# Second layer rebuilt: projections in seven-product pairs through DRAM, memory attention after them, one scan over 64 groups

## The chip, the cores and the metric

The kernel runs on one core of a Trainium2 chip. The metric is the device time of one execution in microseconds (us), lower is better. A core has five engines with instruction streams of their own: TensorE (PE, matmul), VectorE (DVE), ScalarE (ACT), GpSimd (POOL) and SyncE (SP), which here only issues DMAs. Each engine works through its instructions in order, and waits on semaphores for others.

## The reference

Two layers over 1024 tokens of 1024 features, all in fp32. Each layer normalizes, projects, runs a sequence mixer (layer 0 gated linear attention, layer 1 S5) and a four-head cross-attention into 256 memory tokens, gates both with silu(z) and adds the output product to the residual. What the change touches is layer 1:

```python
h = rms_norm(x, norm_w[1])
u, z, xq = split_cols(h @ w_in, [2048, 3072, 1024])
...
# S5: 128 groups of 16 inputs and 64 complex states
x_t = Ab * x_{t-1} + Bb @ u_t            # per group, complex
y_t = Re(C @ x_t)
...
y = gelu(y + d * u)
y = y * sigmoid(y @ w_glu + b_glu)
...
xa = memory_attention(xq, mem_n, w_kv)   # softmax(q k^T / 16) v
x = x + (concat(y, xa) * silu(z)) @ w_out
```

## The kernel before, in words

Activations lie as [feature, token]: a tile has 128 features on the partitions and a half of 512 tokens. A product in fp32 is made of three matmuls on parts of 12 bits, high x high, high x low and low x high (`mm3`). The parts come from `split`: a cast on ACT (L69), which gives the high part, and a subtraction on DVE (L70), which gives the low part. `unit()` loads a block of 128 output features of a weight (128x1024, 512 KB) and splits it; `gemm` then needs 24 matmuls for a half of the tokens.

All DMAs are issued from SP's queue, in one order. The order on each engine and queue comes from a planner: the framework simulates the program when it is built and fixes each engine's order by that; on the chip every engine and queue keeps to it. A tile comes from a pool of a few buffers by tag, and a new tile waits until the readers of the tile that it replaces are done. PSUM has three banks of tag `mm`, two of `a` and one each of `b`, `o` and `s`.

S5 is computed over chunks of eight tokens: 128 chunks. For a group there is an operator from a chunk's inputs to its state (`s5_input_operator`, to `rt_d`), one from inputs to outputs (`s5_operators`, to `tp_d`) and one from the chunk's first state to outputs (`s5_output_operator`, to `o_d`). All are made of POOL instructions mostly; each call covers eight groups. The state goes from chunk to chunk by a scan on DVE of 127 steps.

The stages of the profiled execution, in us from its start:

- 0 to 950: layer 0 up to its output product of the memory branch (`w_out_memory`).
- 950 to 1242: the other two thirds of that product (`w_out`). After each of its blocks `between()` builds one of 16 `s5_operators` and, for n < 8 (`EARLY`), an output operator. `done()` normalizes a half of the tokens for layer 1 and stores them in a permuted order ("p s c": token in the chunk, then chunk).
- 1242 to 1592: `mem_attention` of layer 1. For each head a: two units of queries, two of gates (z), then `each(a)`, which builds four input operators and the late output operators on POOL, and stores them from SP (L743, L763), then scores, softmax and values. The gated output (L321) is stored from SP as well.
- 1592 to 2019: `s5`, in two parts of 64 groups. For each part: inputs `w_su` (eight units, to `ud` in DRAM and back as `uu`), the states before the scan (L835), then the scan (L862 to L866) in two chains of 16 groups, so that one chain's operation lies between two of the other. While part 0 is scanned PE projects the inputs of part 1; while part 1 is scanned it makes the outputs of part 0 (L887, L888). Then outputs of part 1 and the gates `w_sz[0:16]`.
- 2019 to 2651: the GLU, which needs all of S5's outputs (tiles `x200h` and so on), the output product of layer 1, the last norm.

Of the kernel before, what the change touches and what calls it, by code (L numbers as in the profile page):

```python
# [16 lines left out]
P = 128  # L17
# [14 lines left out]
class Tags:  # L32
    """A tile pool for each tag, so that a tile waits for the tiles it replaces and no others."""
# [12 lines left out]
class Trunk:  # L46
# [8 lines left out]
    # ---------------------------------------------------------------- helpers  # L55
# [19 lines left out]
    def unit(self, src):  # L75
        """A block of 1024 weight columns per partition, split into its two 12-bit parts."""
# [7 lines left out]
    def mm3(self, out, ah, al, bh, bl, first, last):  # L84
        mm = self.nc.tensor.matmul
        mm(out, ah, bh, start=first, stop=False)  # L86
        mm(out, ah, bl, start=False, stop=False)  # L87
        mm(out, al, bh, start=False, stop=last)  # L88

    def gemm(self, out, u, xs, first=True, last=True):  # L90
        """out[f, tok] += sum over the eight k tiles of u[k, f] * xs[k][k, tok]."""
        h, l = u
        n = len(xs)
        for k in range(n):
            s = slice(k * P, (k + 1) * P)
            self.mm3(out, h[:, s], l[:, s], xs[k][0], xs[k][1], first and k == 0, last and k == n - 1)

# [15 lines left out]
    def stats(self, pool, xs, width):  # L113
        """1 / RMS over features of xs[k] = [feature, token]."""
# [16 lines left out]
    def rstd(self, pool, tot, width):  # L131
        """From sums of squares, 1 / RMS: by column of 128 tokens, and along tokens over all partitions."""
# [13 lines left out]
    def norm(self, pool, xs, wcol, width, emit):  # L146
        """RMS norm over features: xs[k] is [feature, token]; emit(k, tile) takes the result."""
# [7 lines left out]
    def norm_in_place(self, pool, xs, wcol, width, emit, last):  # L155
        """As norm(), in place, and away from the vector engine unless it's the last one."""
# [92 lines left out]
    def silu2(self, pool, out, ps, tag="zt", bufs=2):  # L249
        """out = 2 * silu(ps)"""  # L250
# [4 lines left out]
    def mem_attention(self, qp, late, pool, kv, wx, wz, xs, y_out, each=lambda a: None):  # L255
        nc = self.nc
        kt = vv = None
        for a in range(4):
            q, z = {}, {}

            def queries(us, hf):
                for f in range(2):
                    ps = self.ps()
                    self.gemm(ps, us[f], xs[hf])
                    q[f, hf] = [qp.tile([P, HALF], F32R, tag="xq" + i, name="xq" + i, bufs=4 if self.layer else 5) for i in "hl"]
# [12 lines left out]
            if a == 0 and self.layer == 1:  # L278
                uz = units(wz)
                gates(uz, 0)  # L280
                gates(uz, 1)
                queries(units(wx), 1)
            else:
                queries(us, 1)
                us = units(wz)
                gates(us, 0)
                gates(us, 1)
            if kt is None:
                kt, vv = kv()
            each(a)  # L290
# [846 lines left out]
```

## Time and profile before

| what | value |
|---|---|
| three runs | 2660.28, 2652.02, 2657.59 us; median 2657.59 |
| the profiled execution | span 2651.5 us, 32793 instructions |
| PE / weight loads | 2479.2 us (94%) / 2058.8 us (78%) |
| DVE / ACT / POOL | 1271.8 (48%) / 846.4 (32%) / 525.7 us (20%) |
| DMA moved | 376.5 MB, mean 142 GB/s |

The profile holds one execution of its own; its span runs from its first to its last instruction, and the median of the three timed runs is 6.1 us above it. The matmuls of PE are pipelined: a record of 0.39 us starts every 0.23 us, so their busy time is the union of the records. "Idle before" in a group is the time in which the engine stood still just before an instruction of the group, and the name behind the arrow is what ended it.

### The profile page before, as it was taken

What the parts mean: (1) busy time and instruction counts of PE and PEld (TensorE: products, weight loads), DVE (VectorE), ACT (ScalarE), POOL (GpSimd) and SP (SyncE); (2) the same over time, 40 slices, a digit from 0 to 9 for tenths busy, and PEclk for the clock granted to TensorE, in tenths of its full rate; (3) what the DMA queues carried; (4) which work ended last, traced back from release to release, by engine and by line L of the source; (5) the groups of instructions that cost most, each with busy time, mean ns of one, the idle gap of its engine ahead of it and who ended that gap; (6) DMA issues with size and microseconds to landing.
All of it is one profiled execution on the core that took longest, in us unless ns stands there. A gap on an engine that the chain in (4) does not pass through costs nothing.

```text
span 2651.5 us, 32793 instructions
## 1 busy us (share of the span) xinstructions
PE 2479.2 (94%) x12000; PEld 2058.8 (78%) x12000; DVE 1271.8 (48%) x3270; ACT 846.4 (32%) x1424; POOL 525.7 (20%) x557
## 2 busy tenths in 40 slices
PE   7999999999999986999997639999999999999998
PEld 6888878888888874777785438888888888888887
DVE  7554353636364533255642211899964222243455
ACT  5422242525253312255421103333234111121144
POOL 6200000000000055676675640000000000000015
PEclk9999999999999997899998779999999999999999
DMA  6612121221213365475453335557668333355434
GB/s 228 188 46 74 52 72 64 74 70 63 81 56 125 114 213 171 140 229 183 165 182 113 124 115 183 167 163 237 220 223 274 123 119 119 119 175 194 136 127 159
DMA packets 198914, 376.50 MB, mean 142 GB/s; under 512 B 17409, under 2 KB 82561, under 8 KB 198753
## 3 DMA queue, kind: packets, MB, share of 16 engines
q1 hardware_dynamic: 198752, 374.41, 43.4%
q8 instruction: 94, 1.54, 0.2%
q14 instruction: 68, 0.55, 0.1%
HBM read 275.12 MB, written 95.55 MB: 140 GB/s over the span
## 4 chain that ended last, share of the span: by engine, by line
PE 33%; DMA 12%; POOL 8%; DVE 6%; issue 3%; SPq 1%; ACT 1%; POOLq 0%; DVEq 0%; ACTq 0%
PE ps_mm L88 10%; PE ps_mm L86 10%; PE ps_mm L87 10%; DMA od<-op 5%; DMA ipw<-ip_d 2%; DVE pd L862 2%; DMA rt<-op 2%; PE ps_a L835 1%; DVE st L866 1%; POOL op L742 1%; DMA par<-in_s_par 1%; POOL op L759 1%; POOL opt L760 1%; DVE pd L864 1%; POOL op L740 1%
## 5 line engine op out<-in xcount | busy, mean ns | idle before, releaser
L86 PE MATMUL ps_mm<-X,wh 128*128 128x512 f32 (+1 forms) x2496 | 970.7, 389 | 32.1 <-ACT X L69 26.9
L88 PE MATMUL ps_mm<-X,wl 128*128 128x512 f32 (+1 forms) x2496 | 968.9, 389 | 5.1 <-DVE wl L70 5.0
L87 PE MATMUL ps_mm<-X,wh 128*128 128x512 f32 (+1 forms) x2496 | 968.7, 388 | 2.6 <-DVE X L70 1.5
L86 PEld LDWEIGHTS ps_mm<-X,wh 128*128 128x128 f32 x2496 | 473.7, 190 | 127.8 <-ACT X L69 28.5
L88 PEld LDWEIGHTS ps_mm<-X,wl 128*128 128x128 f32 x2496 | 473.6, 190 | 100.6 <-DVE wl L70 8.7
L87 PEld LDWEIGHTS ps_mm<-X,wh 128*128 128x128 f32 x2496 | 473.3, 190 | 98.3 <-DVE X L70 5.1
L70 DVE TENSOR_TENSOR wl<-wr,wh 128x1024 fp32r<-128x1024 f32 x258 | 333.6, 1294 | 438.9 <-ACT wh L69 378.9
L69 ACT CAST wh<-wr 128x1024 fp32r<-128x1024 f32 x258 | 271.2, 1051 | 667.9 <-PE ps_mm L87 545.1
L125 POOL TENSOR_TENSOR nacc<-nacc,nsq 128x512 f32<-128x512 f32 (+1 forms) x42 | 56.8, 1353 | 995.6 <-ACT nsq L123 994.8
L862 DVE TENSOR_TENSOR pd<-a,st 128x64 f32<-128x64 f32 x508 | 139.9, 276 | 3.5 <-ACT st L839 1.7
L490 POOL TENSOR_TENSOR rs<-ss,mhalf 128x1 f32<-128x1 f32 x32 | 20.3, 633 | 601.3 <-DVE ss L488 601.3
L252 ACT ACTIVATE zt<-ps_mm 128x512 f32<-128x512 f32 x96 | 57.0, 594 | 233.6 <-PE ps_mm L88 209.3
L253 DVE SCALAR_TENSOR_TENSOR zs<-zt,ps_mm 128x512 f32<-128x512 f32 x96 | 65.3, 681 | 100.1 <-ACT zt L252 98.2
L866 DVE TENSOR_TENSOR st<-st,pd 128x32 f32<-128x32 f32 x508 | 107.4, 212 | 2.0
L70 DVE TENSOR_TENSOR X<-yr,X 128x512 fp32r<-128x512 f32 x96 | 72.4, 780 | 74.9 <-ACT X L69 68.8
L864 DVE TENSOR_TENSOR pd<-pd 128x32 f32<-128x32 f32 x508 | 95.2, 188 | 1.9
L86 PE MATMUL ps_b<-pth,kvh 128*128 128x512 f32 x32 | 14.5, 454 | 86.5 <-DVE y L321 86.0
L321 DVE SCALAR_TENSOR_TENSOR y<-ps_b,zs 128x512 f32<-128x512 f32 x32 | 22.1, 690 | 138.5 <-DMA y<-y 116.4
L69 ACT CAST X<-yr 128x512 fp32r<-128x512 f32 x96 | 58.0, 620 | 92.1 <-DMA yr<-y 76.0
L936 DVE SCALAR_TENSOR_TENSOR sg<-sg,y 128x512 f32<-128x512 f32 x32 | 22.0, 688 | 127.1 <-ACT sg L933 127.1
L86 PEld LDWEIGHTS ps_b<-pth,kvh 128*128 128x128 f32 x32 | 6.7, 211 | 89.3 <-DVE y L321 87.3
L87 PE MATMUL ps_mm<-wl,X 128*128 128x512 f32 x192 | 75.0, 391 | 0.0
(413 smaller groups left out, 3566.6 us busy)
## 6 DMA issues: line engine op xcount, KB each, us to landing
wr<-in_w_out SPq DMA_DIRECT2D x72, 512.0 KB
yr<-y SPq DMA_DIRECT2D x96, 256.0 KB
wr<-in_w_gv SPq DMA_DIRECT2D x32, 512.0 KB
wr<-in_w_glu SPq DMA_DIRECT2D x32, 512.0 KB
wr<-in_w_gz SPq DMA_DIRECT2D x24, 512.0 KB
wr<-in_w_sz SPq DMA_DIRECT2D x24, 512.0 KB
wr<-in_w_k SPq DMA_DIRECT2D x16, 512.0 KB
wr<-in_w_v SPq DMA_DIRECT2D x16, 512.0 KB
```

The lines of the kernel that those rows point to most:

```text
L69: nc.scalar.copy(h, src)
L70: (eng or nc.vector).tensor_tensor(l, src, h.bitcast(F32), ALU.subtract)
L86: mm(out, ah, bh, start=first, stop=False)
L87: mm(out, ah, bl, start=False, stop=False)
L88: mm(out, al, bh, start=False, stop=last)
L125: eng.tensor_tensor(acc[:, :width], acc[:, :width], sq[:, :width], ALU.add)
L252: self.nc.scalar.activation(th, ps, AF.Tanh, scale=0.5)
L253: self.nc.vector.scalar_tensor_tensor(out, th, 1.0, ps, ALU.add, ALU.mult)
L740: nc.gpsimd.tensor_tensor(o, pw[0], c[r], ALU.mult)
L862: v.tensor_tensor(x, a2[:, :, :, g], prev, ALU.mult)
L864: v.tensor_tensor(x[:, :, 0, :], x[:, :, 0, :], x[:, :, 1, :], ALU.add)
L866: v.tensor_tensor(st[part][:, :, g, c], st[part][:, :, g, c], x[:, :, 0, :], ALU.add)
```

## The change

- The tokens of layer 1 are in the permuted order from `w_out_memory` of layer 0 on: its x comes from the host in that order (`xp`), `add_out` reads PSUM with a stride in layer 0 and plainly in layer 1, and the host undoes the order in the output.
- The norm of layer 1 works in place (`layer1_norm`). `combine` forms sums of the quarters of h (two halves of tokens by two halves of features) and splits them.
- `pair` computes two weight blocks by 1024 tokens in seven products in place of eight (each product is four k tiles, 12 matmuls), with four sums of weight quarters on POOL. Thirteen pairs: all of `w_su`, `w_sx[6:8]`, `w_sz[16:24]`. `queries_plain` makes `w_sx[0:6]` as before. All results go to DRAM.
- Input operators and late output operators are built two after each pair. Their stores are issued from POOL's queue in place of SP's.
- Then `memory_attention` runs by itself from what lies in DRAM. `gates_plain` makes `w_sz[0:16]`.
- `s5` computes the states of all groups, one scan over 64 groups on all partitions without a second chain, and then all outputs.

The diff, without docstrings and what stays the same:

```diff
+    def pair(self, pools, w0, w1, x, emit):
+        ws, wq, cp = pools
+        r0 = self.stream.tile([P, 1024], F32, tag="wr", name="wr")
+        nc.sync.dma_start(r0, w0)
+        r1 = wq.tile([P, 1024], F32, tag="wq", name="wq", bufs=2)
+        nc.sync.dma_start(r1, w1)
+        sa, sb = (ws.tile([P, 1024], F32, tag="ws", name="ws", bufs=4) for _ in range(2))
+        a, b = slice(0, HALF), slice(HALF, 1024)
+        g = nc.gpsimd.tensor_tensor
+        g(sa[:, a], r1[:, a], r1[:, b], ALU.add)
+        g(sa[:, b], sa[:, a], r0[:, a], ALU.subtract)
+        g(sb[:, a], r0[:, a], r1[:, a], ALU.subtract)
+        g(sb[:, b], r0[:, b], sa[:, b], ALU.subtract)
...
+        def product(out, u, at, xs, first):
+            for k in range(4):
+                s = slice(at * HALF + k * P, at * HALF + (k + 1) * P)
+                self.mm3(out, u[0][:, s], u[1][:, s], xs[k][0], xs[k][1], first and k == 0, k == 3)
+
+        def keep(ps):
+            c = cp.tile([P, HALF], F32, tag="yr", name="yr", bufs=4)
+            nc.scalar.copy(c, ps)
+            return c
+
+        u = parts(r0, 1024)
+        pu = self.ps()
+        product(pu, u, 0, x["b11"], True)
+        c1 = keep(pu)
+        pv = self.ps("b")
+        product(pv, u, 1, x["b21"], True)
+        emit(0, 0, pv, c1)
+        u = parts(sa, 1024)
+        product(pu, u, 1, x["t2"], False)
+        c2 = keep(pu)
+        pw = self.ps()
+        product(pw, u, 0, x["t1"], True)
+        c5 = keep(pw)
+        u = parts(sb, 1024)
+        product(pu, u, 0, x["t3"], False)
+        emit(1, 1, pu, c5)
+        product(pw, u, 1, x["b22"], False)
+        emit(0, 1, pw, c2)
+        u = parts(r1[:, b], HALF)
+        product(pu, u, 0, x["t4"], False)
+        emit(1, 0, pu, None)
...
     def s5_output_operator(self, pool, powers, n):
...
-            nc.sync.dma_start(od[r], o.rearrange("p g t h -> p g (t h)"))
+            nc.gpsimd.dma_start(od[r], o.rearrange("p g t h -> p g (t h)"))
...
     def s5_input_operator(self, pool, n):
...
-            nc.sync.dma_start(self.rt_d[n]..., o...)
+            nc.gpsimd.dma_start(self.rt_d[n]..., o...)
...
+    def combine(self, tp, xp, x, xs):
...
+        for k in range(4):
+            u, w = x[k], x[k + 4]
...
+            nc.vector.tensor_tensor(sums["t1"], u[:, b], u[:, a], ALU.subtract)
+            nc.vector.tensor_tensor(sums["t2"], w[:, b], sums["t1"], ALU.subtract)
+            nc.gpsimd.tensor_tensor(sums["t3"], w[:, b], u[:, b], ALU.subtract)
+            nc.gpsimd.tensor_tensor(w[:, a], w[:, a], sums["t2"], ALU.subtract)
+            for n in ("t2", "t1", "t3"):
+                h, l = (tp.tile([P, HALF], F32R, tag="T", name="T", bufs=24) for _ in range(2))
+                self.split(h, l, sums[n])
...
+    def projections(self, x1p, tp, x7, xq_d, zs_d, ud, between):
...
+        for j in range(0, 16, 2):
+            self.pair(pools, t["w_su"][j], t["w_su"][j + 1], x7, inputs(j))
+            between()
+        f = self.PLAIN
+        self.pair(pools, t["w_sx"][f], t["w_sx"][f + 1], x7, halves(xq_d, f, False))
+        between()
+        for f in range(16, 24, 2):
+            self.pair(pools, t["w_sz"][f], t["w_sz"][f + 1], x7, halves(zs_d, f, True))
+            between()
...
+    def memory_attention(self, ctx, kv, xq_d, zs_d, y_out):
+        late, pool = self.pool(ctx, "xl1"), self.pool(ctx, "xa1")
+        kt, vv = kv()
+        for a in range(4):
+            for hf in range(2):
...
+                for f in range(2):
+                    nc.sync.dma_start(raw, xq_d[2 * a + f][:, hs])
+                    self.split(*q[f, hf], raw, scale=1.0 / 16)
+                    nc.sync.dma_start(z[f, hf], zs_d[16 + 2 * a + f][:, hs])
+                self.attend(a, hf, kt, vv, q, z, pool, late, y_out)
...
+    def s5(self, ud, y1_d, gates):
+            st = self.pool(ctx, "st").tile([P, 2, 64, P + 1], F32, name="st")
...
+            for j in range(16):
...
+                nc.sync.dma_start(uu, by_step[j])
+                for q in range(2):
...
+                    nc.sync.dma_start(rt, self.rt_d[2 * jl + q][:, 4 * half:4 * half + 4, :])
...
+            for c in range(2, P + 1):
+                pd = sp.tile([P, 2, 2, 64], F32, tag="pd", name="pd", bufs=2)
+                prev = st[:, :, :, c - 1].rearrange("p (o r) g -> p o r g", o=1).broadcast_to([P, 2, 2, 64])
+                v.tensor_tensor(pd, self.a2, prev, ALU.mult)
+                v.tensor_tensor(pd[:, :, 0, :], pd[:, :, 0, :], pd[:, :, 1, :], ALU.add)
+                v.tensor_tensor(st[:, :, :, c], st[:, :, :, c], pd[:, :, 0, :], ALU.add)
+            gates()
+            for jl, half in [(i, h) for i in range(8) for h in range(2)]:
...
     def run(self):
...
+                self.queries_plain(xs1, 0, xq_d)
+                x7 = self.combine(tp, xp, x1, xs1)
+                self.queries_plain(xs1, 1, xq_d)
+                self.combine_last(xp, x1, x7)
+                todo2 = iter([(self.s5_input_operator, (ip, n)) for n in range(16)]
+                             + [(self.s5_output_operator, (ip, powers, n)) for n in range(self.EARLY, 16)])
+
+                def operators():
+                    for _ in range(2):
+                        f, args = next(todo2, (None, ()))
+                        if f:
+                            f(*args)
+
+                self.projections(x1p, tp, x7, xq_d, zs_d, ud, operators)
...
             with ExitStack() as c2:
+                zp = self.pool(c2, "zp")
+                with ExitStack() as c3:
+                    self.memory_attention(c3, self.mem_kv_reload, xq_d, zs_d, y_d[1])
+                self.s5(ud, y1_d, lambda: self.gates_plain(xs1, zp, zs_d))
```

## Rows read from the trace of the kernel before

**Rows 1.** Head of the page: span, and busy time by engine.
```profile
span 2651.5 us, 32793 instructions
...
PE 2479.2 (94%) x12000; PEld 2058.8 (78%) x12000; DVE 1271.8 (48%) x3270; ACT 846.4 (32%) x1424; POOL 525.7 (20%) x557
```

**Rows 2.** Windows by stage: us, busy time by engine, PEclk, DMA share, GB/s.
```profile
950.00:1110.00 160.00, 123.11 (x533) 94.28 (x532) 45.45 (x57) 31.56 (x57) 93.85 (x115) 0.86 0.48 157
1275.00:1592.00 317.00, 226.68 (x1073) 188.64 (x1073) 102.38 (x176) 61.86 (x131) 194.99 (x178) 0.86 0.45 145
1592.00:1797.00 205.00, 205.00 (x1035) 174.56 (x1034) 134.09 (x747) 73.59 (x116) 0.21 (x1) 0.99 0.54 169
1797.00:2019.00 222.00, 218.48 (x1205) 187.35 (x1204) 180.42 (x891) 75.06 (x124) 0.00 (x0) 1.00 0.75 241
```

**Rows 3.** Waits of 1275 to 1592 us: total us, times, longest.
```profile
DVE y L321 <- DMA y<-y: 116.4, 5, 40.5
...
PEld ps_b L86 <- DVE y L321: 87.3, 3, 40.8
```

**Rows 4.** Waits of SP's queue, same stretch.
```profile
SPq L763 <- POOL op L762: 64.8, 27, 9.1
```

**Rows 5.** Waits of 950 to 1110 us.
```profile
ACT X L69 <- DMA yr<-y: 49.4, 11, 15.7
```

**Rows 6.** Timeline of PE: first query and first GLU product (start, us).
```profile
1241.85 0.39 PE L86 MATMUL ps_mm<-X,wh 128*128 128x512 f32 x1
...
2018.57 0.39 PE L86 MATMUL ps_mm<-x200h,wh 128*128 128x512 f32 x1
```

**Rows 7.** Timeline of PE inside a product, 30 matmuls apart.
```profile
1604.42 0.39 PE L86 MATMUL ps_mm<-X,wh 128*128 128x512 f32 x1
...
1611.22 0.39 PE L86 MATMUL ps_mm<-X,wh 128*128 128x512 f32 x1
```

**Rows 8.** Groups by line: busy us, mean ns | idle before, releasers.
```profile
L70 DVE TENSOR_TENSOR wl<-wr,wh 128x1024 fp32r<-128x1024 f32 x258 | 333.6, 1294 | 438.9 <-ACT wh L69 378.9 <-PE ps_a L835 57.6 <-PE ps_mm L88 1.2
L862 DVE TENSOR_TENSOR pd<-a,st 128x64 f32<-128x64 f32 x508 | 139.9, 276 | 3.5 <-ACT st L839 1.7
L866 DVE TENSOR_TENSOR st<-st,pd 128x32 f32<-128x32 f32 x508 | 107.4, 212 | 2.0
L864 DVE TENSOR_TENSOR pd<-pd 128x32 f32<-128x32 f32 x508 | 95.2, 188 | 1.9
L70 DVE TENSOR_TENSOR X<-yr,X 128x512 fp32r<-128x512 f32 x96 | 72.4, 780 | 74.9 <-ACT X L69 68.8 <-PE ps_b L87 5.0 <-PE ps_mm L87 0.8
L253 DVE SCALAR_TENSOR_TENSOR zs<-zt,ps_mm 128x512 f32<-128x512 f32 x96 | 65.3, 681 | 100.1 <-ACT zt L252 98.2 <-DMA zs<-zs 1.8
L125 POOL TENSOR_TENSOR nacc<-nacc,nsq 128x512 f32<-128x512 f32 (+1 forms) x42 | 56.8, 1353 | 995.6 <-ACT nsq L123 994.8
L835 PE MATMUL ps_a<-uu,rtp 128*128 128x128 f32 x256 | 31.1, 275 | 0.0
...
L70 DVE TENSOR_TENSOR atl<-att,ath 128x128 fp32r<-128x128 f32 x32 | 9.2, 289 | 5.9 <-ACT ath L69 5.8
```

**Rows 9.** Tile op of operators: duration ns min/median/max, first and last start.
```profile
L759 POOL TENSOR_TENSOR op<-ipw,ib x32: 1261/1288/2271, 1284.3 to 1554.9; 128x512 f32<-128x512 f32 x32
...
L763 SPq DMA_DIRECT2D rt<-op x32: 319/323/554, 1292.5 to 1570.2; - x32
```

**Rows 10.** Timeline of DVE: maxima of score blocks in layer 1.
```profile
1527.26 0.42 DVE L300 TENSOR_REDUCE nm<-ps_a 128x1 f32<-128x256 f32 x1 [2.40 <-PE ps_a L88]
...
1533.44 0.42 DVE L300 TENSOR_REDUCE nm<-ps_a 128x1 f32<-128x256 f32 x1 [1.62 <-PE ps_a L88]
```

**Rows 11.** Window in the outputs of S5, columns as in rows 2.
```profile
1960.00:2014.00 54.00, 54.00 (x334) 48.16 (x333) 18.22 (x31) 24.22 (x43) 0.00 (x0) 1.00 0.89 283
```

**Rows 12.** Timeline of DVE in a scan, one chain's first two operations.
```profile
1720.06 0.27 DVE L862 TENSOR_TENSOR pd<-a,st 128x64 f32<-128x64 f32 x1
...
1720.37 0.19 DVE L864 TENSOR_TENSOR pd<-pd 128x32 f32<-128x32 f32 x1
```

More of the change, by code (lines that the diff above doesn't have):

```diff
@@ L277, in mem_attention, with attend @@
             queries(us, 0)
[L278 to L287, printed above, removed]
+            queries(us, 1)
+            us = units(wz)
+            gates(us, 0)
+            gates(us, 1)
             if kt is None:
                 kt, vv = kv()
-            each(a)
             for hf in range(2):
+                self.attend(a, hf, kt, vv, q, z, pool, late, y_out)
+    def attend(self, a, hf, kt, vv, q, z, pool, late, y_out):
+        nc = self.nc
+        if True:
+            if True:
                 pt = [self.ps("o"), self.ps("s")]
@@ L541, in w_out @@
             n = c1 - c0
[L542 removed]
+            xs = [[x[:, c0 - hf * HALF:c1 - hf * HALF] for x in hl] for hl in cur[hf]]
             for d in range(8):
@@ new lines, in combine_last, with queries_plain @@
+    def combine_last(self, xp, x, out):
+        for k in range(4, 8):
+            h, l = self.new_x(xp), self.new_x(xp)
+            self.split(h, l, x[k][:, 0:HALF])
+            out["t4"].append((h, l))
+    def queries_plain(self, xs, hf, xq_d):
+        nc, hs = self.nc, slice(hf * HALF, (hf + 1) * HALF)
+        for f in range(self.PLAIN):
+            u = self.unit(self.t["w_sx"][f])
+            ps = self.ps()
+            self.gemm(ps, u, xs[hf])
+            c = self.yr.tile([P, HALF], F32, tag="yr", name="yr", bufs=4)
+            nc.scalar.copy(c, ps)
+            nc.sync.dma_start(xq_d[f][:, hs], c)
@@ new lines, in run @@
+                self.layer = 1
+                for k in range(4):
+                    nc.sync.dma_start(xn_d[k], x1[k][:, HALF:])
+                ip = self.pool(c2, "ip1")
+                tp = self.pool(c2, "T")
+                powers = self.s5_output_powers(ip)
+                self.queries_plain(xs1, 0, xq_d)
[4 more added lines that the diff above has]
+                             + [(self.s5_output_operator, (ip, powers, n)) for n in range(self.EARLY, 16)])
@@ new lines, in operators @@
+                def operators():
[4 more added lines that the diff above has]
+                self.projections(x1p, tp, x7, xq_d, zs_d, ud, operators)
+            for k in range(4):
+                raw = self.yr.tile([P, HALF], F32, tag="yr", name="yr", bufs=4)
+                nc.sync.dma_start(raw, xn_d[k])
+                h, l = self.new_x(xp), self.new_x(xp)
+                self.split(h, l, raw)
+                xs1[1][k] = (h, l)
```

303 lines of the change are left out of this document (161 added, 142 removed).

## The prediction

> **What bounds the kernel now.** I read the page's busy line [rows 1] and the windows by stage first [rows 2]. TensorE (PE) is busy for 2479.2 of 2651.5 us, so the kernel is bound by PE almost everywhere, and the holes are what a change can still win. Two stages hold them: 950 to 1110 us (the output product of layer 0 beside the S5 operators), where PE is busy for 123.1 of 160, and 1275 to 1592 us (the memory attention of layer 1 beside the input operators), where it is busy for 226.7 of 317. From 1592 to 2019 us it is busy for 423.5 of 427: the two scans of the S5 layer run there on VectorE (DVE), each under a product of the other half.
>
> The waits of DVE tell what the 90 us are [rows 3]: the product that gates an attention output waits 116 us in five times for its old tile's store, and PE waits behind it. The store isn't slow; it stands in SP's queue behind stores of operators, and SP is waiting for GpSimd (POOL) to finish those [rows 4]. In the other stage the splits of y wait 49 us for loads in the same queue [rows 5]. So both holes come from one in-order queue that is shared by loads for PE and by stores that POOL finishes late.
>
> The change rebuilds everything from the first query product of layer 1 to the first product of the GLU, 1241.85 to 2018.57 us [rows 6]. That is 776.7 us, and my sum is made against it.
>
> **The change part by part.**
>
> *Queries without pairs.* Six units by two halves, 24 matmuls each. Inside a product 30 matmuls take 6.80 us, 0.2267 us each [rows 7], so 12 x 24 x 0.2267 = 65 us. The norm of the second half and the token sums run beside them: on DVE the sums (8 at about 0.7 us) and 12 split subtractions at 0.78 us, 15 us in all, under the second half's 33 us [rows 8]. They cost nothing while that cover lasts, and up to 15 us without it. I add 5 us for the turn between halves: 70 (65 to 80).
>
> *Projections in pairs.* A pair is seven products of 12 matmuls, 84 in place of 96. Thirteen pairs are 13 x 84 x 0.2267 = 247 us of PE, and save 13 x 12 x 0.2267 = 35. DVE and ACT have 3.5 weight blocks to split for each pair where there were two (3.5 x 1.29 = 4.5 us on DVE, with three additions some 7), which 19 us of PE per pair hide. POOL is another matter. It gets 52 sums of 128x512 at 1.35 us [rows 8], 70 us, and all the operators of 1275 to 1592 us: 178 instructions, all but two of them operators', 195 us [rows 2]. In these 265 us there isn't yet an issue of a store. The 16 input operators make two stores each and the 8 late output operators two each, 48, and they now go out from POOL's own queue. No row shows a DMA issued by POOL. From below I take SP's issue of the same store, 0.32 us; from above the longest that a POOL instruction of an operator took, 2.27 us [rows 9]. Over 48 stores that is 15 to 109 us; I take 0.5 us each, near SP's row since the work is the same, 24 us. Ten more for operator loads that come late: 300 us. Two operators follow each pair (17 us for two input operators, with 5.4 of sums 22.7), and the next pair's sums stand behind them in POOL's order, so for the pairs POOL, with 23 to 25 us each, is slower than PE with 19. If POOL's work can lie wholly outside the pairs, the stage is PE's 247; if issues cost the upper bound, 385.
>
> The Trainium skill, "DMA: Bandwidth & Descriptors", sections "Specifications" and "SWDGE vs HWDGE vs iDMA", says that a DMA issued from GpSimd has its descriptors computed by software on one of that engine's own cores, at about 1 us to the first byte against 0.6 for those that SP issues. No row here shows it. With 1 us of POOL for each of the 48, an estimate from that page, the stage would be 324 and the forecast 2707.
>
> *Memory attention by itself.* Before, its scores and softmax lay between projections; now there are reloaded queries and gates. Two score blocks take 6.18 us from maximum to maximum, where they follow each other [rows 10]; there are 32 blocks, so 16 x 6.18 = 99 us, and about 11 for the reload and split of keys and values ahead of the first: 110. The 16 gate units may fill PE here, which shortens nothing of the chain itself.
>
> *States.* The tile of states of 64 groups is as large as both of before together and takes the place of attention's pools, so they start after attention. Each of 16 blocks loads 512 KB of inputs and twice 256 KB of operators: 16.8 MB. A full stretch of the outputs of before moved 283 GB/s, with the DMA engines busy for 0.89 of it [rows 11]; that makes 60 us (PE alone: the 256 matmuls are 31 [rows 8]).
>
> *One scan.* Before, two scans of 127 steps, in two chains of 16 groups, hid under PE. Now one chain of 64 groups does 127 steps of three dependent operations of 256, 128 and 128 elements. The rows have 276 ns at 64, 188 and 212 ns at 32 [rows 8]; the same kind costs 289 ns at 128, so 96 elements cost 101 ns. That makes 0.478, 0.289 and 0.313 us. A dependent operation starts 0.04 us after the one ahead [rows 12], so a step takes 1.20 us, and 127 take 152. If width cost nothing it would be 102. Sixteen gate units are 16 x 48 x 0.2267 = 174 us of PE and lie over it, but their DVE part (1.29 for the split and twice 0.68 for the gate, 42 us in all) is mixed into the same engine; I count half: 172.
>
> *Outputs.* They need the last step. Each of 16 blocks loads 1.5 MB and stores 0.5: 33.6 MB, at 283 GB/s 119 us; few of the loads can be ahead since tiles have two or three buffers: 115 (PE alone, with twice as many such matmuls as the states: 62). Before, half of it lay under the second scan's products.
>
> *Sum.* 70 + 300 + 110 + 60 + 172 + 115 = 827 us against 776.7: 50 more. The serial part that PE can't fill (attention, states, scan, outputs: 457 us, for which only the 174 us of gates are left) outweighs the 90 us of holes and the 35 us of matmuls that are saved.
>
> *Ahead of it.* In 950 to 1110 us the stores of output operators leave SP's queue, so the loads of y no longer stand behind them. At most the 37 us of idle PE come back, at least nothing (POOL's own issues then delay the operators); POOL's 94 us of work in 160 leave it room, so I take 25. The permuted token order moves a strided read from one add to another, under PE: nothing.
>
> Together 25 us more: 2676.5 us of span. The median of the runs lies 6.1 us above the profiled span, so the prediction is 2683.
>
> **The rivals.**
>
> *POOL doesn't hold the pairs.* Operators depend on nothing that layer 1 computes but their loads, so POOL can start on them under the plain queries, and then 65 us of its 300 are gone when the pairs begin. For it: POOL has only the sums of the second half's norm there. Against it: they are issued after the first pair, and their tiles are few. The projections then take 255 us and the kernel 2638. It decides from a stage below 275 us on, where the whole becomes faster.
>
> *The serial chain is shorter.* Attention at 95 (a split of keys hidden), states at 55, the scan at its 152 (gate work slotted elsewhere), outputs at 100: 402 in place of 457, and 2628. For it: gates can go ahead during attention, which frees DVE in the scan. Against it: loads of two stages follow each other on one queue. Break-even is a chain of 432.
>
> *Issues from POOL are dear.* At 2.27 us each the 48 stores take 109 us of POOL in place of 24, and every sum for the next pair is later: 2768. It decides for more than 25 us of loss from 1 us an issue on. For it: no row excludes it. Against it: the store of SP's row.
>
> *It cancels.* The 25 us of the output product and the hidden operators make up for the chain to within 0.3%, about 8 us, which is what a measurement of this kernel tells from no change.
>
> **How the numbers follow.** The forecast (slower, 2683; its own range 2666 to 2730: below by all 37 us of the stage ahead and queries at 65, above by nothing from that stage and an issue of 0.95 us) has 0.45. POOL free of the pairs has 0.20, the shorter chain 0.15, dear issues 0.13, and cancelling 0.07. Faster is 0.20 + 0.15 = 0.35, the same 0.07, slower 0.45 + 0.13 = 0.58. The range holds both of the faster rivals, also together in part (2638 less 55 is 2583), and dear issues with 17 us of late loads: 2575 to 2785.
>
> **What would show it.** Right: POOL busy for nearly all of the pairs' stage, with PE waiting for splits of the sums; 300 us from the first pair to the first score; then 110, 60, 172 and 115 us, with PE's busy share near half in attention, states and outputs; some 1.2 us per step of the scan. Wrong: PE full in the pairs (POOL was ahead); operators running under the queries; PE holes of 950 to 1110 us as large as before; a scan step far from 1.2 us; outputs at PE's speed, their loads having been ahead. A granted clock below the 0.86 that the two stages with holes have now [rows 2] would lengthen the gates, which I took at full clock. The prediction falls most easily if the planner lets states, gates or operators start in places that I have taken as closed, since half of the sum is work laid end to end.

## The result, and the profile after

The changed kernel takes 2881.03 us (median of four runs) where the kernel before takes 2656.92: ratio 1.0834, 95% interval 1.0808 to 1.0859. The forecast was slower, at 2683: the way was right, but 224 us were lost where 25 were forecast.

The page of the changed kernel: span, busy time by engine, the DMA queues, and the lines of the chain that ended last.

```profile
span 2880.3 us, 31868 instructions
...
PE 2485.7 (86%) x11844; PEld 2052.2 (71%) x11844; DVE 1334.0 (46%) x2224; ACT 890.8 (31%) x1502; POOL 661.1 (23%) x680
...
q0 software_dynamic: 19456, 16.90, 2.0%
...
PE ps_mm L86 49%; DMA od<-op 8%; DMA ipw<-ip_d 3%; PE ps_b L86 3%; DVE pd L1025 3%; DMA ow<-od 2%; DVE st L1027 2%; PE ps_a L86 2%; DVE pd L1026 1%; PE ps_o L86 1%; POOL op L792 1%; POOL opt L812 1%; PE ps_a L1017 1%; PE ps_a L1049 1%; DMA par<-in_s_par 1%
```

PE's busy time is nearly that of before [rows 1], so almost all of the 229 us of span are idle PE; q0 is new and holds what POOL now issues, 16.9 MB. The windows tell where (columns as in [rows 2]): the output product of layer 0; queries; pairs; from the last pair to the first score; attention; states; scan; outputs.

```profile
950.00:1110.00 160.00, 123.21 (x527) 93.88 (x526) 55.07 (x58) 31.90 (x57) 105.92 (x129) 0.85 0.51 157
...
1243.00:1340.00 97.00, 78.64 (x319) 62.34 (x318) 72.36 (x56) 32.51 (x51) 71.02 (x59) 0.91 0.63 194
1340.00:1661.00 321.00, 255.54 (x1042) 203.92 (x1042) 139.47 (x100) 77.90 (x110) 241.94 (x218) 0.90 0.49 149
1661.00:1698.00 37.00, 7.30 (x31) 5.59 (x29) 13.58 (x14) 9.49 (x14) 14.14 (x12) 0.64 0.59 187
1698.00:1838.00 140.00, 138.97 (x719) 119.05 (x720) 77.22 (x169) 50.48 (x117) 0.33 (x1) 0.97 0.46 153
1838.00:1937.00 99.00, 99.00 (x568) 86.65 (x567) 16.98 (x20) 51.85 (x84) 0.00 (x0) 1.00 0.71 230
1937.00:2120.00 183.00, 21.60 (x98) 18.01 (x97) 169.53 (x389) 6.89 (x10) 0.00 (x0) 0.57 0.06 20
2120.00:2239.00 119.00, 78.03 (x505) 69.52 (x504) 12.67 (x30) 36.48 (x64) 0.00 (x0) 0.90 0.83 270
```

Two stages stand out. In the scan PE is busy for 21.6 of 183 us: the gates that were to lie there are done, and attention and states, where PE is full, are where they went. And between the last pair and the first score PE does nothing for 30 of 37 us. What ends that hole is a wait of attention for POOL's tiles; the scan's is one wait of PE. Waits of 1661 to 1838 us (DVE), of 1245 to 1690 us (POOL), and of 1937 to 2125 us (PE):

```profile
DVE xql L73 <- DMA od<-op: 21.0, 1, 21.0
...
POOL op L792 <- DMA od<-op: 64.8, 13, 7.0
POOL op L811 <- DMA ipw<-ip_d: 41.4, 17, 13.9
...
PE ps_a L1049 <- ACT xg L1043: 161.4, 1, 161.4
```

Attention's query tile `xql` waits for the store of an operator, with which it has nothing to do: it takes the memory of the operators' tiles. So attention starts behind POOL's last operator here, wherever PE stands.

Groups of the scan, and of two operations that DVE does beside POOL:

```profile
L1025 DVE TENSOR_TENSOR pd<-a,st 128x256 f32<-128x256 f32 x127 | 78.5, 618 | 5.5 <-ACT st L1021 1.2
L1027 DVE TENSOR_TENSOR st<-st,pd 128x128 f32<-128x128 f32 x127 | 49.1, 386 | 4.2
L1026 DVE TENSOR_TENSOR pd<-pd 128x128 f32<-128x128 f32 x127 | 37.1, 292 | 4.4
...
L70 DVE TENSOR_TENSOR wl<-ws,wh 128x1024 fp32r<-128x1024 f32 x26 | 67.6, 2599 | 13.2 <-ACT wh L69 13.0
L928 DVE TENSOR_TENSOR ub<-ps_mm,yr 128x512 f32<-128x512 f32 x18 | 12.4, 692 | 41.1 <-PE ps_mm L86 27.1 <-issue 10.4 <-DMA ud<-ub 3.6
```

The tile in which POOL forms the operators, and its stores (duration min/median/max in ns, first and last start): the last one is issued at 1682.9 us, and the first score follows 15 us later.

```profile
L795 POOL DMA_DIRECT2D od<-op x32: 835/835/997, 959.9 to 1682.9; - x32
...
L815 POOL DMA_DIRECT2D rt<-op x32: 580/580/662, 1263.5 to 1528.9; - x32
```

### The profile page after: what moved, and what is told of

The parts are those of the page before. It is cut to its first block, busy times and chain, and to the rows that moved or that the text cites. A ratio compares the mean times of both kernels' runs of the same rounds, so it can differ in the third digit from the quotient of the medians.

```text
span 2880.3 us, 31868 instructions
## 1 busy us (share of the span) xinstructions
PE 2485.7 (86%) x11844; PEld 2052.2 (71%) x11844; DVE 1334.0 (46%) x2224; ACT 890.8 (31%) x1502; POOL 661.1 (23%) x680
## 4 chain that ended last, share of the span: by engine, by line
PE 59%; DMA 16%; POOL 9%; DVE 8%; ACT 3%; issue 3%; SPq 1%; POOLq 0%; DVEq 0%; ACTq 0%
PE ps_mm L86 49%; DMA od<-op 8%; DMA ipw<-ip_d 3%; PE ps_b L86 3%; DVE pd L1025 3%; DMA ow<-od 2%; DVE st L1027 2%; PE ps_a L86 2%; DVE pd L1026 1%; PE ps_o L86 1%; POOL op L792 1%; POOL opt L812 1%; PE ps_a L1017 1%; PE ps_a L1049 1%; DMA par<-in_s_par 1%
## 5 line engine op out<-in xcount | busy, mean ns | idle before, releaser
L86 PE MATMUL ps_mm<-X,wh 128*128 128x512 f32 (+1 forms) x4472 | 1379.6, 389 | 44.6 <-ACT X L69 21.6
L86 PEld LDWEIGHTS ps_mm<-X,wh 128*128 128x128 f32 x4472 | 838.9, 190 | 220.4 <-ACT X L69 23.8
L86 PE MATMUL ps_mm<-X,wl 128*128 128x512 f32 (+1 forms) x2236 | 866.8, 388 | 12.2 <-DVE wl L70 12.2
L1049 PE MATMUL ps_a<-xg,ow 128*128 128x128 f32 x256 | 57.4, 313 | 191.8 <-ACT xg L1043 161.4
L86 PE MATMUL ps_mm<-T,wh 128*128 128x512 f32 x312 | 104.8, 419 | 37.2 <-ACT yr L133 37.2
L86 PE MATMUL ps_mm<-wh,X 128*128 128x512 f32 x384 | 125.0, 392 | 0.0
L86 PEld LDWEIGHTS ps_mm<-T,wh 128*128 128x128 f32 x312 | 62.3, 203 | 55.3 <-ACT yr L133 42.7
L312 ACT ACTIVATE zt<-ps_mm 128x512 f32<-128x512 f32 x80 | 47.6, 595 | 143.0 <-PE ps_mm L86 142.7
L86 PEld LDWEIGHTS ps_mm<-wh,X 128*128 128x128 f32 x384 | 72.0, 188 | 14.9
L86 PE MATMUL ps_mm<-T,wl 128*128 128x512 f32 x156 | 65.9, 422 | 18.8 <-DVE wl L70 18.8
L1025 DVE TENSOR_TENSOR pd<-a,st 128x256 f32<-128x256 f32 x127 | 78.5, 618 | 5.5 <-ACT st L1021 1.2
```

Of the source, the lines that this page charges most:

```text
L86: self.nc.tensor.matmul(out, a, b, start=start, stop=stop, skip_group_check=True)
L312: self.nc.scalar.activation(th, ps, AF.Tanh, scale=0.5)
L1025: v.tensor_tensor(pd, self.a2, prev, ALU.mult)
L1049: nc.tensor.matmul(o, ow[:, g], xg[:, g], start=False, stop=True)
```

## The experiments

Three theories were held against each other. A: the scan is uncovered, since the planner put the gates ahead of it. B: the pairs lost the time, by POOL and by DVE beside it. C, formed from the first results: the chain from POOL's operators over states and scan to the outputs sets the middle of both kernels, and PE's holes there are its slack. Times and ratios are medians against the kernel before; windows and waits come from one profiled execution of each kernel.

### Where the gates run

**late_gates**: the gates' temporaries get the two buffers of a tag `gz`, which the last block of states uses first for its operators, so no gate can be finished before that.
```diff
-                    rt = sp.tile([P, 4, P], F32, tag="rtp", name="rtp", bufs=3)
+                    tag = "gz" if j == 15 else "rtp"
+                    rt = sp.tile([P, 4, P], F32, tag=tag, name=tag, bufs=2 if j == 15 else 3)
...
-                self.silu2(zp, z, ps, bufs=1)
+                self.silu2(zp, z, ps, tag="gz")
```


> The 16 gate units are held back until the last block of states is done, so that they can only run under the scan. Theory A (the scan is uncovered, because the gates ran ahead of it, in attention and states, where they lengthened the chain): PE's idle time during the scan falls from 161 us to under 60, attention and states together from 274 to about 190 us, the scan stage grows by up to the gates' 42 us on DVE; in all 2790 to 2850 us. Theory B (the loss lies in the projections, where POOL and DVE hold the pairs): 2870 to 2890.

Measured: 2826.8 us, 1.0639 (1.0599 to 1.0679). Windows from the first score on: attention, states, scan, outputs.

```profile
1698.00:1784.00 86.00, 74.82 (x424) 61.57 (x423) 60.14 (x148) 37.46 (x99) 0.32 (x1) 0.98 0.53 179
1784.00:1845.00 61.00, 41.40 (x256) 38.31 (x256) 0.14 (x1) 36.70 (x64) 0.00 (x0) 0.84 0.84 282
1845.00:2058.00 213.00, 162.13 (x707) 132.18 (x708) 199.83 (x430) 36.14 (x51) 0.00 (x0) 0.89 0.24 79
2058.00:2170.00 112.00, 71.39 (x503) 62.17 (x501) 12.69 (x30) 36.09 (x63) 0.00 (x0) 0.97 0.87 285
```

Attention and states fall from 239 to 147 us, the scan grows by 30, the GLU starts 69 us earlier. A holds, for 54 of 224 us by the medians; the profiled execution was the fastest of the four of late_gates, and shows 69.

**two_parts**: `s5` in two halves, in the order states(0), scan(0), states(1), scan(1), outputs(0), gates, outputs(1), with the gates held as above. The scan of one half:
```diff
-                pd = sp.tile([P, 2, 2, 64], F32, tag="pd", name="pd", bufs=2)
+                pd = sp.tile([P, 2, 2, 32], F32, tag="pd", name="pd", bufs=2)
```


> The changed kernel with two scans of 32 groups instead of one of 64, states and outputs of a half beside the scan of the other, and the gates held back until the first half's states are done. If it is the form of the single scan that lost the time: towards 2720, since the outputs of the first half are then covered. If what is missing is work to lay under a scan, in whatever form (the inputs are all projected by then): two scans of 0.9 us a step are 230 us where one took 182, and with the gates' 42 us of DVE they take back what the covered outputs give: 2790 to 2840, as with late gates alone (2827).

Measured: 2808.0 us, 1.0566 (1.0538 to 1.0594), 19 better than late_gates by the medians. The two scans take 297 us (1822 to 2119). PE is busy for 128 of 128 us up to 1950 and for 85 of the 169 behind it. So the form of the scan alone doesn't give the time back: gates, states and the first outputs fill one scan and half of the other, and the products that are left wait for the scan.

### POOL, SP and the pairs

**no_ops**: leaves out the arithmetic and the loads of the 16 input operators and, in the same way, of the eight late output operators; the stores stay.
```diff
     def s5_input_operator(self, pool, n):
+        for i in range(2):
+            nc.gpsimd.dma_start(self.rt_d[n][:, 4 * i:4 * i + 4].rearrange("p a b -> p (a b)"), self.blank)
+        return
```


> The arithmetic and the loads of the 16 input operators and of the eight late output operators are left out; their 48 stores stay on POOL's queue, with a constant tile. Theory A: the stage of the pairs falls from 321 us to about 270 (PE's 247 and its waits for copies), and all else stays: about 2830. Theory B: the projections lose their whole excess over PE's time, queries too: 2780 or less.

Measured: 2800.6 us (one run). The pairs take 253 us (PE busy 240), 68 less, attention's first query is split at 1618 instead of 1688 us, and the GLU starts 82 us earlier. From there to the GLU it is about as long as before (539 us against 551). So operators cost the pairs and the turn to attention together some 80 us, more than theory A expected and less than B.

**plain13**: plain products in place of the pairs; the token sums of `combine` go with them.
```diff
     def pair(self, pools, w0, w1, x, emit):
+        for i, w in enumerate((w0, w1)):
+            u = self.unit(w)
+            for hf in range(2):
+                ps = self.ps()
+                self.gemm(ps, u, x[hf])
+                emit(i, hf, ps, None)
```


> The 13 pairs computed by plain products again (96 matmuls in place of 84, no token sums, no weight sums on POOL, no copies out of PSUM between products), all else as in the changed kernel. If the pairs are worth their 35 us of matmuls: 2890 to 2920. If their copies, sums and the DVE time beside POOL cost as much as they save: 2860 to 2890. Theory B (pairs are what went wrong): below 2840.

Measured: 2850.8 us, 1.0736 (1.0717 to 1.0755): 30 us faster without the pairs, which none of the three cases had. POOL loses its sums, issues its last operator store at 1600.9 instead of 1682.9 us, and attention starts at 1667; PE's 35 us more of matmuls fit into time in which it waited. Here attention starts 66 us behind POOL's last store, and no wait for POOL stands before it, so the products set its start.

**after_oploads**
```diff
-            nc.sync.dma_start(b.rearrange("p g r x -> p (g r x)"), src)
+            nc.gpsimd.dma_start(b.rearrange("p g r x -> p (g r x)"), src)
```
The loads of `pw` and `c` move in the same way.

> The changed kernel with the operators' loads on POOL's queue too. With no operator arithmetic the pairs took 253 us in place of 321. If what cost the 68 us is SP's queue, held 193 us by operator loads so that stores of projected tiles come late and DVE waits 81 us for them: the pairs fall to 270 to 285 us, and the kernel to 2835 to 2850. If it is DVE's splits, stretched from 1.3 to 2.6 us beside POOL: no change or, with 40 us more of issues on POOL, slower: 2875 to 2910.

Measured: 2887.5 us, 1.0865 (1.0836 to 1.0895). In the changed kernel SP waits for POOL at the operators' loads in 1340 to 1661 us, DVE waits for stores in SP's queue, and PE for copies and splits; no wait of PE, ACT or DVE for POOL's sums is among them:

```profile
SPq L804 <- POOL opt L812: 101.1, 21, 10.4
SPq L784 <- POOL opt L793: 92.2, 5, 20.6
...
DVE ub L950 <- DMA zs<-ub: 55.6, 4, 24.1
...
PE ps_mm L86 <- ACT yr L133: 37.2, 13, 18.6
PE ps_mm L86 <- DVE wl L70: 18.8, 5, 8.2
```

Without that the pairs take 254 us, and the rest of the time until the first score waits (windows of this kernel):

```profile
1321.00:1575.00 254.00, 240.62 (x1044) 194.38 (x1043) 148.35 (x100) 78.26 (x110) 230.95 (x221) 1.00 0.59 175
1575.00:1728.00 153.00, 65.91 (x282) 53.51 (x280) 31.84 (x30) 23.20 (x32) 77.90 (x74) 0.72 0.38 110
```

What ends that wait, in DVE's waits of 1575 to 1880 us:

```profile
DVE xql L73 <- DMA od<-op: 73.4, 1, 73.4
```

The 86 us that the pairs gave back are all spent on waiting for POOL, whose last store is now issued at 1717.8. The cause of slow pairs is SP's queue, held by loads into tiles that POOL still reads: the splits of the sums on DVE are nearly as slow here as there (2366 against 2590 ns in the pairs), PE waits for 13 us in place of 66, and the pairs ran at PE's pace. But the pairs weren't what the kernel waited for.

**after_mix**
```diff
-                todo2 = iter([(self.s5_input_operator, (ip, n)) for n in range(16)]
-                             + [(self.s5_output_operator, (ip, powers, n)) for n in range(self.EARLY, 16)])
+                todo2 = iter([x for n in range(8) for x in (
+                    (self.s5_input_operator, (ip, 2 * n)), (self.s5_output_operator, (ip, powers, 8 + n)), (self.s5_input_operator, (ip, 2 * n + 1)))])
```


> The changed kernel with the order of the operators changed: two input operators and one late output operator in turn, instead of 16 input operators and then eight output operators. Theory C: attention takes the memory of the operators' tiles, so it starts after POOL's last store; at the end POOL waits 65 us for output operators' stores to land, one after the other; mixed, these lie under the input operators, POOL ends up to 50 us earlier and so does all behind it: 2830 to 2860. If PE's products and not POOL set the start of attention: 2870 to 2890.

Measured: 2879.3 us, 1.0835 (1.0812 to 1.0858): nothing. POOL still waits 93 us for `od` stores in the whole kernel (112 before this edit), and its last store is issued at 1684.8. The order alone doesn't shorten its chain, so this run doesn't test what an earlier end would give.

**after_early16**
```diff
-    EARLY = 8
+    EARLY = 16
```


> The changed kernel with all 16 output operators built beside the output product of layer 0 instead of eight there and eight after the pairs. POOL's last store then lies some 165 us earlier. If POOL's tail sets when attention starts (in every variant so far it started within 20 us of POOL's last store): attention starts at the end of the pairs, 1640 us or so, and the kernel takes 2820 to 2850, unless the output product of layer 0 ends later for it. If the pairs set it: 2870 to 2885.

Measured: 2896.6 us, 1.0909 (1.0886 to 1.0931). The output product now ends some 50 us later (its window of 1110 to 1250 us has PE busy for 108 of 140), the pairs begin at 1406, and attention starts at 1697 as before, though POOL's last store is issued at 1628.0: as in plain13, products that came late set it. Work that POOL does earlier is work that PE waits for there.

**after_best** (late_gates, after_oploads and after_mix together) and **after_early16_best** (late_gates, the input operators' loads on POOL's queue, and `EARLY = 16`):

> The changed kernel with the mixed order, all operator DMAs on POOL's queue, and the gates held back until the states are done. Pairs end at about 1580 us, POOL at about 1625, then attention 120, states 58, scan with gates 211, outputs 113: the GLU would start at about 2127 and the kernel end at 2740 to 2800, still behind the kernel before. If something else holds attention back: above 2800.

> The changed kernel with all output operators early, input operators' loads on POOL's queue, and the gates held back until the states are done: pairs end at 1580 us, attention at 1700, states at 1760, scan with gates at 1970, outputs at 2083, end at 2725. 2700 to 2760, still slower than before: the chain behind the projections alone is 500 us, with 174 us of PE to lay under it.

Measured: 2802.1 us, 1.0549 (1.0528 to 1.0571), and 2829.5 us, 1.0642 (1.0618 to 1.0666). In after_best the pairs end at 1580 as expected, but POOL's last store is issued at 1690 and not at 1625, `xql` waits 59 us for POOL, and PE is busy for 32 of the 120 us behind the pairs. In after_early16_best, 70 us above its expectation, attention starts at 1696 us, and from there to the GLU it takes 488 us, near the 472 of late_gates. What stays over the kernel before is, by this, POOL's chain up to attention and the serial part behind it.

### The kernel before: what is its hole worth?

**before_poolq**
```diff
-            nc.sync.dma_start(od[r], o.rearrange("p g t h -> p g (t h)"))
+            nc.gpsimd.dma_start(od[r], o.rearrange("p g t h -> p g (t h)"))
```
The store to `rt_d` moves in the same way.

> The kernel before with one part of the change alone: the stores of both kinds of S5 operators are issued from POOL's queue instead of SP's. By the prediction's reading of the holes (the stores of attention outputs stand behind operator stores in SP's queue) the 90 us of 1275 to 1592 mostly close, and some of the 37 us of 950 to 1110: 2560 to 2620. Rival: the hole of 950 to 1110 stayed at 37 us in the changed kernel, so the queue was not what held it, and POOL pays 0.6 to 0.8 us for an issue: 2640 to 2670.

Measured: 2675.6 us, 1.0076 (1.0061 to 1.0092). The hole stays. Waits of DVE and of SP in 1242 to 1620 us:

```profile
DVE y L321 <- DMA y<-y: 111.4, 5, 54.7
...
SPq L752 <- POOL opt L760: 183.9, 29, 10.4
SPq L732 <- POOL opt L741: 62.7, 6, 11.8
```

The stores of operators left SP's queue, and SP waits at their loads (L752, L732) instead. The prediction had named the stores alone [rows 4]. Yet among SP's waits in the stretch of rows 4, 1275 to 1592 us of the kernel before, a load stands ahead of that store:

```profile
SPq L752 <- POOL opt L760: 67.5, 30, 7.5
```

**before_yact**
```diff
-                    nc.sync.dma_start(y_out[16 + 2 * a + f][:, hf * HALF:(hf + 1) * HALF], y)
+                    (nc.scalar if self.layer else nc.sync).dma_start(y_out[16 + 2 * a + f][:, hf * HALF:(hf + 1) * HALF], y)
```


> The kernel before, with the stores of layer 1's attention outputs issued from ACT's queue instead of SP's; nothing else. With only the operator stores moved, DVE still waited 111 us for these stores, since SP was held for 184 us by operator loads that wait for POOL to free their tiles. If the place of the output stores in SP's queue makes the hole of 1275 to 1592 us: DVE's wait for its old tile disappears, and most of PE's 86 us with it: 2570 to 2610. If the weights and inputs that stand in the same queue are then late instead: 2630 to 2660.

Measured: 2653.7 us, 0.9992 (0.9980 to 1.0004). DVE's wait is gone, but PE's hole shrinks by 15 us only, in which PE gets just 8 matmuls further: it now waits 43 us for the softmax, and ACT in its order for the stores it issues.

**before_opq**: the loads as in after_oploads and the stores as in before_poolq.

> The kernel before with all DMAs of the two kinds of operators, loads too, on POOL's queue. SP then never waits for POOL. If SP's queue is what holds the attention outputs: 2570 to 2610, as with the output stores on ACT. Against it: some 120 issues at 0.6 to 0.8 us are 85 us more of POOL in the stage, 280 us of 317, and the states then wait for late operators: 2620 to 2660.

Measured: 2659.0 us, 1.0009 (0.9995 to 1.0022). Windows of that kernel, three stages of [rows 2]:

```profile
1275.00:1592.00 317.00, 314.88 (x1504) 263.48 (x1502) 120.13 (x183) 79.64 (x156) 228.63 (x251) 1.00 0.55 162
1592.00:1797.00 205.00, 147.93 (x772) 126.90 (x772) 111.53 (x638) 59.52 (x95) 37.05 (x40) 0.86 0.50 160
1797.00:2019.00 222.00, 184.62 (x1017) 158.83 (x1015) 181.18 (x983) 65.43 (x108) 0.00 (x0) 0.94 0.67 217
```

SP's longest wait in 1560 to 1680 us:

```profile
SPq L832 <- POOL opt L741: 58.4, 1, 58.4
```

PE's 90 us of idle time are closed and come back as 57 and 37 us in the next two stages: the states' operators (L832) are loaded into tiles that wait for POOL's last operator, as attention's do in the changed kernel. That operator is stored 68 us later than in the kernel before (1643.1 us), of which before_poolq, where only the stores moved, has 64 (1639.7).

**before_op5**, **before_opq_op5**: five operator tiles in the kernel before and in before_opq.
```diff
-            o = pool.tile([P, HALF], F32, tag="op", name="op", bufs=3)
+            o = pool.tile([P, HALF], F32, tag="op", name="op", bufs=5)
```


> The kernel before with five buffers instead of three for the tile in which POOL forms an operator (in both stages that build them); nothing else. Theory C (what sets the end of this stretch is the chain POOL's operators, states, scans, outputs; PE's holes are its slack, since closing them all left the time where it was): POOL waits 64 us for its own stores to land in 1242 to 1592, and with these gone states and scan begin 20 to 50 us earlier: 2605 to 2640. If SP's queue, which loads and stores the operators in order, sets POOL's pace whatever the buffers: 2645 to 2660.

> All DMAs of operators on POOL's queue and five operator tiles. There the PE hole was closed (315 of 317 us busy) and the time was the same, 2659. Theory C: now POOL's remaining waits for stores (57 us) go as well, states begin by as much earlier, and it's the faster of the two: 2600 to 2630. If POOL's own issues (0.6 to 0.8 us each) eat that: 2645 to 2660.

Measured: 2651.9 us, 0.9988 (0.9978 to 0.9999), POOL now waiting 60 us for loads instead of 27; and 2645.9 us, 0.9962 (0.9949 to 0.9975), with POOL's last store at 1633.4 instead of 1643.1 us.

**before_first** (in the kernel before) and **before_opq_first** (in before_opq_op5):
```diff
-                    for n in range(4 * a, 4 * a + 4):
-                        self.s5_input_operator(ip, n)
-                        if n >= self.EARLY:
-                            self.s5_output_operator(ip, powers, n)
+                    for n in range(8 * a, 8 * a + 8) if a < 2 else range(4 * a, 4 * a + 4):
+                        if a < 2:
+                            self.s5_input_operator(ip, n)
+                        else:
+                            self.s5_output_operator(ip, powers, n)
```


> The kernel before with the order of its operators alone changed: all 16 input operators at the first two heads, the eight late output operators at the last two (before: each output operator behind the input operator of its number). Theory C, that the chain operators, states, scans sets the end of this stretch: the states need input operators alone, so they and the scan could begin some 60 us earlier; but in this kernel the last projections of the states' inputs stand behind PE's hole, so only where SP lets PE through: 2600 to 2640. If SP's queue holds both alike: 2645 to 2660.

> All operator DMAs on POOL's queue, five operator tiles, and all input operators first. With the queue alone PE's hole closed and came back, 90 us of it, behind late operators; with them first, the states begin as soon as their inputs are there. Theory C: PE stays full from 1275 to 2019 us and the kernel takes 2560 to 2610. If what returned is another wait (scans, outputs): 2630 to 2650.

Measured: 2635.7 us, 0.9918 (0.9903 to 0.9933), and 2628.3 us, 0.9893 (0.9871 to 0.9916), the fastest of all, though above the 2610 that theory C gave it. The states don't begin 60 us earlier, since their tiles still wait for POOL's last output operator (L832 waits 45 us in before_opq_first); but against before_opq_op5 that one is done earlier. POOL's last store and the first step of the scan (rows of the tile's issues and of the scan: count, duration, first and last start), in before_first and then in before_opq_first:

```profile
L743 SPq DMA_DIRECT2D od<-op x32: 478/496/1245, 956.5 to 1557.0; - x32
L862 DVE TENSOR_TENSOR pd<-a,st x508: 262/276/287, 1648.8 to 1942.5; 128x64 f32<-128x64 f32 x170
```

```profile
L743 POOL DMA_DIRECT2D od<-op x32: 812/841/880, 963.5 to 1620.8; - x32
L862 DVE TENSOR_TENSOR pd<-a,st x508: 259/272/284, 1663.4 to 1946.7; 128x64 f32<-128x64 f32 x170
```

In the kernel before and its three variants with the stores on SP's queue the scan starts 88 to 92 us after POOL's last store (1575.3 and 1666.6 us in the kernel before), in the four with the stores on POOL's queue 42 to 47 us after it. So the scan moves with POOL's end in all eight. In the four on POOL's queue the states' loads wait for POOL. In the kernel before and in before_first POOL's end also ends PE's hole: the last attention stores (L322) stand in SP's queue behind the last operator store, and PE's wait behind them ends 15 us after that store in both. From there to the scan PE is busy for 76 us. The end of that wait in the kernel before, then in before_first (timeline of PE):

```profile
1590.00 0.80 PE L86 MATMUL ps_b<-pth,kvh 128*128 128x512 f32 x1 [40.35 <-DVE y L321]
```

```profile
1572.07 0.80 PE L86 MATMUL ps_b<-pth,kvh 128*128 128x512 f32 x1 [39.69 <-DVE y L321]
```

So what moves the scan is POOL's end. The time follows the scan where PE's hole is open (before_first: scan 18 us earlier, kernel 23; before_poolq: 20 later, 19 more). Where the hole is closed it is 16 to 27 us better than the scan's start alone would make it (before_opq: scan 19 later, time 3 more; before_opq_first: scan 3 earlier, time 30 less). So, as an estimate that takes the scan's start to set the rest, some 20 of the 90 us of hole are worth time.

## Why the prediction was wrong

By its own steps, on the profiled span: 2880.3 us against the 2676.5 of the sum, 204 more.

- **The stage ahead**: 25 us were to come back in 950 to 1110 us. None did: PE is busy for 123.2 us there, as before. The step failed with the reading of the queue: the loads of y stand behind operator *loads* too, for which SP waits 27.5 us here, and POOL waits 47.6 us for its own stores. The splits' wait for y fell from 49.4 to 43.4 us only. (after_oploads, with those loads off SP, has PE busy for 138.8 of these 160.) 25 us.

```profile
SPq L784 <- POOL opt L793: 27.5, 3, 12.7
```

- **Queries**: 97 us, where 70 were summed and 80 was the bound. DVE is busy for 72 of the 97, so the cover for the token sums may have been too thin: plain13, which forms none, issues its last query store 8 us earlier (1331 against 1339). With the operators' loads off SP (after_oploads) the query stores, first to last, span 81 us in place of 91. The rest stays open. 27 us.
- **Pairs**: 300 us were summed by POOL's work, and from the first pair to the first score it took 358. That POOL's end and not PE's sets this stage was right, but the path was not the one given. The pairs were to wait for their sums, which stand behind operators in POOL's order; the waits show none for sums, SP's queue slowed the pairs, and without that they ran at PE's pace (after_oploads). What makes POOL's end count is attention's tiles, a wait that the prediction doesn't have. POOL's issues measured 0.58 and 0.84 us, near the value taken. The mis-sized term is "ten more for operator loads that come late": from the first pair on POOL waited 65 us for the stores of output operators, which the term left out, and 18 for loads. Against it, 8 of the 32 stores of input operators were issued by 1340 us, under the queries: 47 us of POOL's work that the 300 had in the pairs. The chain named the wait for stores before the change: the page of the kernel before had 5% of the span there.

```profile
PE ps_mm L88 10%; PE ps_mm L86 10%; PE ps_mm L87 10%; DMA od<-op 5%; DMA ipw<-ip_d 2%; DVE pd L862 2%; DMA rt<-op 2%; PE ps_a L835 1%; DVE st L866 1%; POOL op L742 1%; DMA par<-in_s_par 1%; POOL op L759 1%; POOL opt L760 1%; DVE pd L864 1%; POOL op L740 1%
```

- **Gates**: the step that failed most. The 174 us of gates were laid over the scan, and "may fill PE here, which shortens nothing" was said of attention. The planner did fill attention and states with them, so that these took 140 and 99 us in place of 110 and 60, and nothing was left for the scan. With the gates held back the two take 86 and 61 (late_gates), and the kernel gains 54 us by the medians. 69 us over the sum on this span.
- **Scan**: 1.43 us a step (182 us for 127) in place of 1.20. The gates' DVE time wasn't in it, so its 172 for the stage came near by two errors. The width was priced from a row of dense operands. The additions without a stride came out as said (292 ns for 289), but the two operations that read the state with a stride of 129 elements took 618 and 386 where 478 and 313 were summed, 1.8 ns for each element more: (618 - 276) / 192 and (386 - 212) / 96. No run has the same operations without the stride.
- **Outputs**: 119 us for 115. Right, and by the cause given: 270 GB/s.
- From the GLU on, the span is 8 us longer than before; not followed up.

Together 25 + 27 + 58 + 69 + 11 + 4 + 8 = 202 us.

Of the rivals, "POOL doesn't hold the pairs" came true in its condition, a quarter of the input operators under the queries, but not in its time; "the serial chain is shorter" went the other way (541 us in place of 457); dear issues didn't occur. What came true was named only as what would make the prediction fall: a planner that starts gates where the prediction had taken the place as closed.

The prediction also set the 90 us of holes against the serial part as time that a change can win. That entered no term of its sum, which adds up stages. But before_opq closed the hole and gained nothing, with POOL's end 68 us later; by the estimate above some 20 of the 90 were to be had. In this stretch the kernel before hangs on POOL's chain, which also ends PE's hole, with the scan behind it; a change that gives POOL more work, and the scan less cover, is slower by both. Shown: the gates' place (late_gates), SP's queue as cause of the slow pairs (after_oploads), POOL's tiles as what attention and states wait for (the waits of the changed kernel, after_oploads and before_opq). Only argued: what the hole alone is worth, and why POOL's end stayed at 1683 to 1690 us when its order was changed.

## What to carry to other kernels

An idle PE is worth its time only if PE is what the next stages wait for: close the hole first, alone, and see whether the end moves. Work that is free to run (gates) goes where a greedy planner first finds a gap, not where cover is needed; if it's meant to cover a later serial stage, something must hold it back. And a pool that takes another's memory is a dependency on the other's slowest engine: read the waits for tiles that share no data.

## What the runs showed of the hardware

- DVE's operations with two operands in SBUF stretch beside POOL, and those with one in PSUM don't: `wl<-ws,wh` took 2599 ns (mean) beside POOL's operators and 1399 ns in no_ops, `ub<-ps_mm,yr` 692 and 691. The Trainium skill, "GPSIMD Engine Reference", section "1. Specifications", says that GpSimd shares its SBUF interfaces with VectorE and that they contend for instructions with two SBUF inputs; the traces agree.
- A DMA of 256 KB issued by POOL held it for 580 ns (`rt`) or 835 ns (`od`, in runs of 512 bytes), where SP's issues took 323 and 534 in the kernel before (medians); an `od` store from POOL landed 9.9 us after its issue (median), an `rt` store 3.2.
